# The entry of the gate products: pair 2 moved ahead of the fourth activation sums

## The chip, the cores and the metric

One core of a Trainium2 chip runs the whole kernel as one program. The metric is the device time of one execution in microseconds (us). Five engines matter here: TensorE (PE, with its weight loads as PEld), VectorE (DVE), ScalarE (ACT), GpSimd (POOL), and SyncE (SP), which issues nearly every DMA. Each engine takes its instructions in the order of its own queue.

## The reference

One layer of a hybrid block over 1024 latent tokens and 256 context tokens, all in float32:

```
h  = rms_norm(x, g_pre) * (1 + scale) + shift            # 1024 x 1024
q, k, v, g_a, u_f, g_f, c_a, c_b, g_c, s_a, s_f, s_c = split(h @ w_in)
y_a = (attention(q, k, v, context) * silu(g_a)) @ p_attn
y_f = ((fourier_mix(u_f) @ w_four) * silu(g_f)) @ p_four
y_c = (conv_module(c_a, c_b) * silu(g_c)) @ p_conv
merged = sigmoid(s_a) * y_a + sigmoid(s_f) * y_f + sigmoid(s_c) * y_c
x + gate * rms_norm(merged @ w_out, g_post)
```

The change lies in the products that give the gate columns `s_a`, `s_f`, `s_c`, `g_a`, `g_f`, `g_c`.

## The kernel before

**Split products.** Every float32 operand is written as a high part and a low part (`split`, line 93: ACT casts the high part, DVE or POOL subtracts it to get the low part). A product is then three matmuls per 128 rows of depth: high by high, high by low, low by high (`mm3`, lines 141 to 143).

**Gate pairs.** After the attention stage, the remaining gate columns are computed in twelve pairs, numbered from 0. A pair is 256 columns of `w_in` (two raw tiles of 512 KB, `raw`), and its product with `h` is a 2 by 2 block product done with seven half-size products in place of eight. Each of the seven, `p1` to `p7`, is twelve matmuls of 128x512. They use sums of blocks on both sides:

- on the weight side `prep_a` splits blocks a11 and a12 (tiles `c0`), `wsum(n, 0..3)` forms four sums `w0` to `w3` (line 1283; on POOL for pairs 2 to 11, on DVE for pairs 0 and 1), `prep_b` splits w0 and w1 (tiles `c1`), `prep_c` splits w2 and w3 (tiles `c2`), `prep_d` splits a22 (tile `c3`);
- on the activation side the sums t0 to t3 are formed once for all pairs by `h_sums` and, for the fourth sum set that only `p4` reads, by `h_last` (lines 1243 and 1244). `h_split` splits them. While they wait they are kept in the buffer `mg`.

**Steps of a pair.** `p1` makes bank x and copies it out on ACT (s1, line 1318); `p2` makes bank y; `p6` and then `p7` add onto bank x, each copied out by DVE (u2, u3, line 1320); `p5` makes bank z, copied out by ACT (s5, line 1318), and `p3` adds onto bank z; `p4` makes bank w. Since `p6` adds onto the bank that the s1 copy reads, and `p3` onto the bank that the s5 copy reads, each waits for its copy. The gates `g2`, `g3`, `g4`, `g7` add the pieces on DVE (line 1346), take a tanh on ACT (line 1325, two buffers `th`) and store it by DMA (`thd`).

**Order.** The order on all five engines is that in which the code is written. From pair 3 on a loop emits one pair after another, with the next pair's weights prepared in between. The first three pairs are written out by hand, since the activation sums are formed and split in between. `raws(n)` issues the two loads of a pair's raw tiles, which have two buffers, so they can only start when the former pair's raw tiles have been read for the last time. Six loads of 512 KB (`mg[r]` from `fcd`, line 1483) bring branch results back into `mg` when the sums there have been used up; they too go through SP.

Of the kernel before, what the change touches and what calls it, by code (L numbers as in the profile page):

```python
# [52 lines left out]
def block_kernel(ctx: ExitStack, tc: tile.TileContext, x, ctxt, cvec, cctx, wmodt, wgate,  # L53
                 rows2, cols, w_in, rpbp, w_four, w_pw, pst, w_out, masks, bdc, bds, dcos, dsin, out):
    nc = tc.nc
    pe, act, dve, pool, sp = nc.tensor, nc.scalar, nc.vector, nc.gpsimd, nc.sync
# [35 lines left out]
    def split(src, hi, lo, lo_eng=None):  # L92
        return act.copy(hi, src), (lo_eng or pool).tensor_tensor(out=lo, in0=src, in1=f32(hi), op=ALU.subtract)  # L93
# [10 lines left out]
    def emit_raw(i):  # L104
        while state["raw"] <= min(i, len(wq) - 1):
            e = wq[state["raw"]]
            t = wp.tile([P, e[1], e[2]], F32, tag="raw", bufs=2, name=f"raw{state['raw']}")
            sp.dma_start(t, e[0])
            e[3] = t
            state["raw"] += 1  # L110

    def emit_split(i):
        while state["spl"] <= min(i, len(wq) - 1):
            j = state["spl"]
            emit_raw(j)
            e = wq[j]
            if e[6] == 0:
                state["spl"] += 1
                continue
            e[4] = wp.tile([P, e[1], e[2]], F32R, tag="whi", name=f"whi{j}")  # L120
            e[5] = wp.tile([P, e[1], e[2]], F32R, tag="wlo", name=f"wlo{j}")
            for i in range(e[6]):
                ks = slice(i * e[1] // e[6], (i + 1) * e[1] // e[6])
                lo = e[7][i % len(e[7])] if e[7] else state.get("lo")
                ops = split(e[3][:, ks], e[4][:, ks], e[5][:, ks], lo)
                for op, prev in zip(ops, held):
                    after(op, prev)
            state["spl"] += 1
# [45 lines left out]
    for what in border:  # L174
        n = int(what[1])
# [13 lines left out]
    for what in sum(plan, []) + ["s1"]:  # L189
        n = int(what[1])  # L190
# [136 lines left out]
    def h_split(k, h, eng=None):  # L327
        split(h32s.pop((k, h)), hh[k][:, H[h]], hl[k][:, H[h]], eng)
# [496 lines left out]
    raws = {}  # L825
# [322 lines left out]
    for i in range(NU + 4):  # L1148
        n = i % 16
# [60 lines left out]
    def slot(i, name):  # L1210
        return gp.tile([P, T], F32R, tag=f"g{i}", name=name)
# [12 lines left out]
    def parts(k):  # L1224
        return [[f32(v) for v in bop[i][k]] for i in ((1, 1), 1, (2, 1), (2, 2))]
# [14 lines left out]
    def h_last(k):  # L1240
        b21, l21 = parts(k)[2]
        t2 = ts[4, k] = ts[2, k]
        dve.tensor_tensor(out=t2, in0=b21, in1=t2, op=ALU.subtract)
        dve.tensor_tensor(out=t2, in0=t2, in1=l21, op=ALU.add)  # L1244
# [6 lines left out]
    NP = len(pairs)  # L1251

    def wtile(nm):
        return [wp.tile([P, KT, P], F32R, tag=t, name=nm) for t in ("whi", "wlo")]

    def put(n, name, src, hl_, j):
        dst = [v[:, 4 * j:4 * j + 4] for v in hl_]
        split(src, *dst, dve)
        ops[n, name] = dst

    def blocks(n):
        if n >= NP:
            c0, c1 = ((n - NP + 4 * i) * P for i in range(2))
            return (mgt[0][:, :, c0:c0 + P], mgt[1][:, :, c0:c0 + P],
                    mgt[0][:, :, c1:c1 + P], mgt[1][:, :, c1:c1 + P])
        r0, r1 = (wq[i][3] for i in pairs[n][2])
        return r0[:, 0:4], r0[:, 4:8], r1[:, 0:4], r1[:, 4:8]

    def prep_a(n):
        if n < NP:  # L1270
            emit_raw(pairs[n][2][1])
        a11, a12, _, _ = blocks(n)
        c0 = wtile(f"c0{n}")
        put(n, "a11", a11, c0, 0)
        put(n, "a12", a12, c0, 1)

    def wsum(n, i):
        a11, a12, a21, a22 = blocks(n)
        i0, i1, op = ((a21, a22, ALU.add), (ops.get((n, 0)), a11, ALU.subtract), (a11, a21, ALU.subtract),
                      (a12, ops.get((n, 1)), ALU.subtract))[i]  # L1280
        t = swp.tile([P, 512], F32, tag="sw", name=f"w{i}")
        t = t.rearrange("p (k c) -> p k c", k=4)
        (pool if 1 < n < NP else dve).tensor_tensor(out=t, in0=i0, in1=i1, op=op)  # L1283
        ops[n, i] = t

    def prep_b(n, which=(0, 1)):
        if (n, "c1") not in ops:
            ops[n, "c1"] = [slot(12 + i, f"c1{n}").rearrange("p (k c) -> p k c", k=8) for i in range(2)]
        for i in which:
            put(n, f"s{i + 1}", ops[n, i], ops[n, "c1"], i)  # L1290

    def prep_c(n, which=(0, 1)):
        if (n, "c2") not in ops:
            ops[n, "c2"] = wtile(f"c2{n}")
        for i in which:
            put(n, f"s{3 + i}", ops[n, 2 + i], ops[n, "c2"], i)

    def prep_d(n):
        c3 = (slot(15 if n == 1 else 14, f"c3{n}") if n < NP else hp.tile([P, T], F32R, tag="hh7", name=f"c3{n}"))
        c3 = c3.rearrange("p (k c) -> p k c", k=8)  # L1300
        c3 = c3[:, 0:4], c3[:, 4:8]
        put(n, "a22", blocks(n)[3], c3, 0)

    def raws(n):
        emit_raw(pairs[n - 1][2][1] + 2)
# [112 lines left out]
    for i in (0, 1, 3, 2):  # L1418
        wsum(0, i)
# [8 lines left out]
    def stack_load():  # L1428
        for k in range(8):
            for t, s in zip((hh, hl), H):  # L1430
                sp.dma_start(f32(t[k][:, H[0]]), fcd[k][:, s])

    def stack_in(*ks):
        for k in ks:
            gh.append(slot(order[2 * k], f"gh{k}"))
            gl.append(slot(order[2 * k + 1], f"gl{k}"))
        for t, s in zip((hh, hl), H):
            for k in ks:
                split(f32(t[k][:, H[0]]), gh[k][:, s], gl[k][:, s], dve)

    def go(n, *what):
        for w in what:
            step(n, w)
# [12 lines left out]
    go(0, "p6")  # L1456
    h_split(3, 2, 3)
    wsum(1, 0)
    wsum(1, 1)
    go(0, "p5")  # L1460
    prep_b(1, (1, 0))
# [4 lines left out]
    raws(2)  # L1466
    go(1, "p6", "g2")
    prep_c(1)
    h_last(0)
    go(1, "p5")  # L1470
    h_last(1)
    h_split(4, 0, 1)
    go(0, "g3")
    h_last(2)
    h_last(3)
    h_split(4, 2, 3)
    go(1, "p7")
    prep_a(2)
    go(0, "g7")
    go(1, "p3", "g3")  # L1480
    go(2, "p1", "p2")
    for r in (6, 7, 4, 5, 0, 1):
        sp.dma_start(mg[r], fcd[r])
    wsum(2, 0)
    wsum(2, 1)
    go(0, "p4", "g4")
    prep_b(2)
    go(1, "p4", "g7", "g4")
    prep_d(2)
    wsum(2, 2)  # L1490
    wsum(2, 3)
    prep_c(2)
    raws(3)
    for n in range(2, NP):
        more = n + 1 < NP
        go(n, *("p1", "p2")[2 * (n == 2):], "g2")
        if more:
            prep_a(n + 1)
            wsum(n + 1, 0)
            wsum(n + 1, 1)  # L1500
        else:
            stack_load()
        go(n, "p4")
        if more:
            prep_d(n + 1)
        else:
            stack_in(0, 1, 2)
        go(n, "p6")
        if more:
            wsum(n + 1, 2)  # L1510
            wsum(n + 1, 3)
            raws(n + 2)
        else:
            stack_in(3)
            state["lo"] = dve
            emit_split(i_p[0])
        go(n, "p5")
        if more:
            prep_b(n + 1)
        else:  # L1520
            stack_in(4)
        go(n, "p7", "g7", "g4")
        if not more:
            stack_in(5)
        go(n, "p3", "g3")
        if more:
            prep_c(n + 1)
# [228 lines left out]
    n = NP  # L1756
# [136 lines left out]
```

## Time and profile before

| | |
|---|---|
| median of three runs | 961.87 us (960.55 to 963.34) |
| the profiled execution | 959.82 us, of which the span between the first and last instruction is 958.0 us |
| busy PE / DVE / ACT / POOL | 888.4 / 754.6 / 428.2 / 386.5 us |
| mean granted TensorE clock | 0.98 of full speed |

The span is what the rows below are timed in, from its first instruction on. A busy PE is a PE with a matmul in flight; how fast those go is read from the granted clock beside it.

### The profile page before, as it was taken

The page shows a single profiled execution, that of the slowest core. Times are in us where ns is not written, and L with a number is a line of the kernel's source. Part 1 is how long each engine was busy: PE and PEld are TensorE (multiplying, and loading weights), DVE is VectorE, ACT ScalarE, POOL GpSimd, SP SyncE. Part 2 cuts the span into 40 slices and gives each one's busy share as a digit, 9 for nine tenths or more (in the row PEclk, how much of TensorE's full clock was granted, in tenths as well). Part 3 has the DMA queues.
Part 4 walks back from the last instruction along what each step waited for, and adds up shares of the span by engine and source line. Part 5 has one row for each costly group of instructions (what it writes and reads, how often), then busy time and mean ns, then how long its engine had stood idle before and what let it go on. Part 6 is the DMA issues. An engine that isn't in the chain of part 4 may idle for free. (4 is left out here: it accounts for less than half of the span.)

```text
span 958.0 us, 13133 instructions
## 1 busy us (share of the span) xinstructions
PE 888.4 (93%) x4560; PEld 741.2 (77%) x4560; DVE 754.6 (79%) x1204; ACT 428.2 (45%) x855; POOL 386.5 (40%) x334
## 2 busy tenths in 40 slices
PE   5886999989799999999999968999999999998896
PEld 3655899978578988888888856888778888875685
DVE  5999398989668999999958775447874579998985
ACT  6661522232346767767642433433343430224442
POOL 3694732155214444444520022416653037671232
PEclk9998999999899999999999979999999999999999
DMA  9613123244534454535422246423331599853323
GB/s 354 255 52 104 44 89 134 84 152 125 159 88 123 143 152 130 156 122 144 133 79 88 68 122 216 134 89 99 110 99 44 195 350 327 303 187 110 110 88 132
DMA packets 114308, 136.38 MB, mean 142 GB/s; under 512 B 5697, under 2 KB 83777, under 8 KB 114242
## 3 DMA queue, kind: packets, MB, share of 16 engines
q1 hardware_dynamic: 114098, 134.95, 43.3%
q0 software_dynamic: 144, 0.59, 0.3%
q8 instruction: 36, 0.59, 0.3%
q14 instruction: 30, 0.25, 0.1%
HBM read 102.55 MB, written 29.36 MB: 138 GB/s over the span
## 5 line engine op out<-in xcount | busy, mean ns | idle before, releaser
L141 PE MATMUL ps<-hh,whi 128*128 128x512 f32 x304 | 128.4, 422 | 4.6 <-DVE kst L564 3.7
L143 PE MATMUL ps<-hh,wlo 128*128 128x512 f32 x304 | 120.6, 397 | 0.0
L142 PE MATMUL ps<-hl,whi 128*128 128x512 f32 x304 | 120.4, 396 | 0.0
L93 POOL TENSOR_TENSOR wlo<-raw,whi 128x512 fp32r<-128x512 f32 (+2 forms) x52 | 84.1, 1635 | 77.9 <-ACT whi L93 77.9
L93 DVE TENSOR_TENSOR c<-w,c 128x512 fp32r<-128x512 f32 x64 | 52.8, 862 | 34.4 <-ACT c L93 34.3
L1639 POOL TENSOR_TENSOR mg<-mg,th 128x512 f32<-128x512 f32 x30 | 50.5, 1686 | 62.4 <-DVE th L1636 60.9
L93 ACT CAST whi<-raw 128x512 fp32r<-128x512 f32 (+2 forms) x65 | 43.7, 704 | 66.8 <-PE ps L142 33.5
L141 PEld LDWEIGHTS ps<-hh,whi 128*128 128x128 f32 x304 | 58.7, 193 | 15.2 <-issue 4.6
L1030 POOL TENSOR_TENSOR bias<-mk,braw 128x288 f32<-128x288 bf16 (+1 forms) x64 | 54.1, 847 | 38.4 <-DVE mn L1062 38.4
L143 PEld LDWEIGHTS ps<-hh,wlo 128*128 128x128 f32 x304 | 58.0, 191 | 13.1
L142 PEld LDWEIGHTS ps<-hl,whi 128*128 128x128 f32 x304 | 58.7, 193 | 9.9 <-issue 0.5
L1095 ACT CAST pt<-tp 96x384 fp32r<-96x384 f32 (+1 forms) x96 | 46.1, 514 | 42.9 <-PE tp L1088 42.2
L1283 POOL TENSOR_TENSOR w<-raw 128x512 f32<-128x512 f32 x10 | 16.0, 1601 | 107.0 <-DVE mg L1244 50.3
L1101 DVE TENSOR_TENSOR pt<-tp,pt 96x384 fp32r<-96x384 f32 (+1 forms) x96 | 54.5, 594 | 2.6 <-ACT pt L1095 1.2
L1062 DVE CUSTOM_DVE_ANT_0 pr<-scb,bias 128x544 f32<-128x544 f32 (+1 forms) x64 | 49.4, 772 | 8.5 <-PE scb L1055 7.7
L1069 ACT ACTIVATE pr<-pr,mn 128x544 f32<-128x544 f32 (+1 forms) x64 | 50.8, 794 | 3.7 <-DVE mn L1062 3.6
L143 PE MATMUL ps<-gh,wlo 128*128 128x512 f32 x128 | 50.0, 390 | 0.8 <-DVE wlo L93 0.8
L141 PE MATMUL ps<-gh,whi 128*128 128x512 f32 x128 | 50.2, 392 | 0.0
L142 PE MATMUL ps<-gl,whi 128*128 128x512 f32 x128 | 49.9, 390 | 0.2 <-DVE gl L93 0.2
L1088 PE MATMUL tp<-ident,pr 128*128 128x128 f32 (+1 forms) x320 | 45.8, 274 | 1.4 <-DVE rc L1075 1.0
L93 ACT CAST c<-w 128x512 fp32r<-128x512 f32 x64 | 37.1, 617 | 21.3 <-DVE w L1283 21.1
L1076 DVE TENSOR_SCALAR pr<-pr,rc 128x544 f32<-128x544 f32 (+1 forms) x64 | 41.7, 652 | 2.3
(498 smaller groups left out, 2701.6 us busy)
## 6 DMA issues: line engine op xcount, KB each, us to landing
raw<-in_w_in_dram SPq DMA_DIRECT2D x51, 512.0 KB
wt<-in_wmodt_dram SPq DMA_DIRECT2D x16, 512.0 KB
thd<-th SPq DMA_DIRECT2D x32, 256.0 KB
th<-thd SPq DMA_DIRECT2D x32, 256.0 KB
braw<-in_rpbp_dram SPq DMA_DIRECT2D x32, 192.0 KB
vt<-vd SPq DMA_DIRECT2D x48, 128.0 KB
vd<-vs SPq DMA_DIRECT2D x20, 256.0 KB
vt<-vd SPq DMA_DIRECT2D x48, 96.0 KB
```

The costliest lines, as they stand in the source:

```text
L93: return act.copy(hi, src), (lo_eng or pool).tensor_tensor(out=lo, in0=src, in1=f32(hi), op=ALU.subtract)
L141: pe.matmul(ps, wh, mh, start=start, stop=False, **kw)
L142: pe.matmul(ps, wh, ml, start=False, stop=False, **kw)
L143: pe.matmul(ps, wl, mh, start=False, stop=stop, **kw)
L1030: pool.tensor_tensor(out=dst, in0=mk[:, a * 3 + MJ[j], 0:n].rearrange("p (r w) -> p r w", w=W), in1=raws[h_, min(j, 1)][:, :, 0:W], op=ALU ...
L1062: dve.tensor_tensor_reduce(out=pr, in0=sc, in1=biases[h_][:, FULL[h_](n)], scale=1.0, scalar=BIG, op0=ALU.add, op1=ALU.min, accum_out=mn)
L1069: act.activation(pr, pr, AF.Exp, scale=-1.0, bias=mn, accum_out=sums)
L1076: dve.tensor_scalar(out=pr, in0=pr, scalar1=rc, scalar2=None, op0=ALU.mult)
L1088: pe.transpose(tp[0:(kw if b < 3 else P), b], src, ident)
L1095: act.copy(pt[0:q, b0:b1, 0], tp[0:q, b0:b1])
L1101: dve.tensor_tensor(out=pt[0:q, b0:b1, 1], in0=tp[0:q, b0:b1], in1=f32(pt[0:q, b0:b1, 0]), op=ALU.subtract)
L1639: eng.tensor_tensor(out=mg[d][:, s], in0=mg[d][:, s], in1=t, op=ALU.add)
```

## The change

Three things are done to the stretch between the pair 1 products and pair 3.

- The splits of pair 2 (`prep_a(2)`, then w0, w1 and `prep_b(2)`) move ahead of `h_last` for the fourth activation sums and of `h_split(4, ...)`.
- `p1`, `p2`, `p6` and `p5` of pair 2 move ahead of `p4` of pairs 0 and 1. The rest of pair 2 follows (`p7`, `p4`, `p3`), and its weight preparation and that of pair 3 are written out by hand. The loop starts at pair 3.
- The four weight sums of pair 2 move from POOL to DVE.

No arithmetic is added or removed: the count of matmuls, splits and DMAs is the same.

```
--- before.py
+++ after.py
@@ -1280,7 +1280,7 @@
                       (a12, ops.get((n, 1)), ALU.subtract))[i]
         t = swp.tile([P, 512], F32, tag="sw", name=f"w{i}")
         t = t.rearrange("p (k c) -> p k c", k=4)
-        (pool if 1 < n < NP else dve).tensor_tensor(out=t, in0=i0, in1=i1, op=op)
+        (pool if 2 < n < NP else dve).tensor_tensor(out=t, in0=i0, in1=i1, op=op)
         ops[n, i] = t
 
     def prep_b(n, which=(0, 1)):
@@ -1466,34 +1466,48 @@
     raws(2)
     go(1, "p6", "g2")
     prep_c(1)
+    prep_a(2)
     h_last(0)
     go(1, "p5")
+    wsum(2, 0)
+    wsum(2, 1)
     h_last(1)
+    go(0, "g3")
+    go(1, "p7")
+    prep_b(2, (1, 0))
     h_split(4, 0, 1)
-    go(0, "g3")
+    go(0, "g7")
+    go(1, "p3", "g3")
     h_last(2)
     h_last(3)
+    go(2, "p1", "p2")
     h_split(4, 2, 3)
-    go(1, "p7")
-    prep_a(2)
-    go(0, "g7")
-    go(1, "p3", "g3")
-    go(2, "p1", "p2")
+    go(1, "g7")
     for r in (6, 7, 4, 5, 0, 1):
         sp.dma_start(mg[r], fcd[r])
-    wsum(2, 0)
-    wsum(2, 1)
-    go(0, "p4", "g4")
-    prep_b(2)
-    go(1, "p4", "g7", "g4")
-    prep_d(2)
+    go(2, "p6", "g2")
     wsum(2, 2)
     wsum(2, 3)
+    go(2, "p5")
     prep_c(2)
+    go(0, "p4")
+    prep_d(2)
     raws(3)
-    for n in range(2, NP):
+    go(0, "g4")
+    go(1, "p4", "g4")
+    go(2, "p7")
+    prep_a(3)
+    go(2, "p4", "g7", "g4")
+    for i in range(4):
+        wsum(3, i)
+    prep_d(3)
+    prep_b(3)
+    raws(4)
+    go(2, "p3", "g3")
+    prep_c(3)
+    for n in range(3, NP):
         more = n + 1 < NP
-        go(n, *("p1", "p2")[2 * (n == 2):], "g2")
+        go(n, "p1", "p2", "g2")
         if more:
             prep_a(n + 1)
             wsum(n + 1, 0)
```

**ScalarE, from the splits of w2, w3 of pair 1 on.** In the names, `c21` are the tiles of w2, w3 of pair 1, `c02` the splits of a11, a12 of pair 2, `c12` those of its w0, w1, `t40` and `t41` the high parts of the fourth activation sums, `s1`, `s5` the copies of banks x and z, and `th` a tanh. Before:

```order
L93 CAST c21_6081<-w2_6052 128x512
L93 CAST c21_6081<-w3_6054 128x512
L1318 COPY s5_6102<-z_6089 128x512
L93 CAST t40_5715<-mg1_5697 128x512 x2
L1325 ACTIVATE th_6112<-u2_6009 128x512
L93 CAST t41_5716<-mg0_5696 128x512 x2
L93 CAST c02_6137<-raw35_6059 128x512 x2
L1318 COPY s5_6143<-z_6019 128x512
L1325 ACTIVATE th_6146<-s5_6143 128x512
L1325 ACTIVATE th_6162<-u2_6075 128x512
L1318 COPY s1_6178<-x_6165 128x512
L1325 ACTIVATE th_6217<-u3_6050 128x512
```

and now:

```order
L93 CAST c21_6081<-w2_6052 128x512
L93 CAST c21_6081<-w3_6054 128x512
L93 CAST c02_6087<-raw35_6059 128x512 x2
L1318 COPY s5_6108<-z_6095 128x512
L1325 ACTIVATE th_6118<-u2_6009 128x512
L93 CAST c12_6135<-w1_6112 128x512
L93 CAST c12_6135<-w0_6110 128x512
L93 CAST t40_5715<-mg1_5697 128x512 x2
L1318 COPY s5_6145<-z_6019 128x512
L1325 ACTIVATE th_6148<-s5_6145 128x512
L1325 ACTIVATE th_6164<-u2_6075 128x512
L1318 COPY s1_6184<-x_6171 128x512
```

The splits of pair 2 (`c02`, and now `c12` too) have moved up past both splits `t40` and `t41`. The copy of pair 2's bank x (`s1_6178` before, `s1_6184` now) still stands behind the same two tanhs, the last row of the second piece; ahead of them now also stand the `c12` splits.

**VectorE, at the same place.** `mg1` here holds the fourth activation sums, `c02` and `c12` are the low parts of the splits, `w0` and `w1` pair 2's weight sums, and `u2_6009` is the sum for the gate `g3` of pair 0. Before:

```order
L93 TENSOR_TENSOR c21_6082<-w2_6052,c21_6081 128x512
L93 TENSOR_TENSOR c21_6082<-w3_6054,c21_6081 128x512
L1243 TENSOR_TENSOR mg1_5697<-hh4_87,mg1_5697 128x512
L1244 TENSOR_TENSOR mg1_5697<-mg1_5697,hl4_95 128x512
L1243 TENSOR_TENSOR mg1_5697<-hh5_88,mg1_5697 128x512
L1244 TENSOR_TENSOR mg1_5697<-mg1_5697,hl5_96 128x512
L93 TENSOR_TENSOR t42_5717<-mg1_5697,t40_5715 128x512 x2
L1346 TENSOR_TENSOR u2_6009<-u2_6009,z_6019 128x512
L1346 TENSOR_TENSOR u2_6009<-u2_6009,v_5930 128x512
L1243 TENSOR_TENSOR mg0_5696<-hh6_89,mg0_5696 128x512
L1244 TENSOR_TENSOR mg0_5696<-mg0_5696,hl6_97 128x512
```

and now:

```order
L93 TENSOR_TENSOR c21_6082<-w3_6054,c21_6081 128x512
L93 TENSOR_TENSOR c02_6088<-raw35_6059,c02_6087 128x512 x2
L1243 TENSOR_TENSOR mg1_5697<-hh4_87,mg1_5697 128x512
L1244 TENSOR_TENSOR mg1_5697<-mg1_5697,hl4_95 128x512
L1283 TENSOR_TENSOR w0_6110<-raw36_6061 128x512
L1283 TENSOR_TENSOR w1_6112<-w0_6110,raw35_6059 128x512
L1243 TENSOR_TENSOR mg1_5697<-hh5_88,mg1_5697 128x512
L1244 TENSOR_TENSOR mg1_5697<-mg1_5697,hl5_96 128x512
L1346 TENSOR_TENSOR u2_6009<-u2_6009,z_6019 128x512
L1346 TENSOR_TENSOR u2_6009<-u2_6009,v_5930 128x512
L1320 COPY u3_6133<-x_5961 128x512
L93 TENSOR_TENSOR c12_6136<-w1_6112,c12_6135 128x512
```

Between the splits of pair 1 and the additions into `u2_6009` there now stand the two low parts of `c02` and the two weight sums, while the second half of the fourth sums (`mg0`) and its splits have moved behind.

**TensorE, at the end of `p2` of pair 2** (bank y). `t40` and `t42` are the fourth activation sums, `t20` and `t22` the second ones. Before:

```order
L141 MATMUL y_6180<-hh7_90,c02_6137 128x512
L142 MATMUL y_6180<-hl7_98,c02_6137 128x512
L143 MATMUL y_6180<-hh7_90,c02_6138 128x512
L141 MATMUL w_6203<-t40_5715,c30_5887 128x512
L142 MATMUL w_6203<-t42_5717,c30_5887 128x512
L143 MATMUL w_6203<-t40_5715,c30_5887 128x512
```

and now:

```order
L141 MATMUL y_6186<-hh7_90,c02_6087 128x512
L142 MATMUL y_6186<-hl7_98,c02_6087 128x512
L143 MATMUL y_6186<-hh7_90,c02_6088 128x512
L141 MATMUL x_6171<-t20_5707,c12_6135 128x512
L142 MATMUL x_6171<-t22_5709,c12_6135 128x512
L143 MATMUL x_6171<-t20_5707,c12_6136 128x512
```

Where `p4` of pair 0 (bank w) stood behind `p2`, there now stands `p6` of pair 2, which adds onto bank x of `p1`.

## Rows read from the trace of the kernel before

**Rows 1.** Windows: stretch, us, then busy time of PE, PEld, DVE, ACT, POOL; clock, DMA.
```profile
558.60:566.10 7.50, 0.04 (x1) 0.00 (x0) 7.31 (x10) 2.42 (x5) 3.44 (x3) 0.65 0.09 35
566.10:571.10 5.00, 4.80 (x11) 3.31 (x11) 3.17 (x6) 2.19 (x4) 0.00 (x0) 0.50 0.17 60
...
584.80:588.20 3.40, 3.40 (x10) 2.62 (x9) 0.92 (x2) 0.63 (x1) 0.00 (x0) 0.50 1.03 296
...
640.00:700.00 60.00, 59.56 (x262) 48.72 (x261) 44.98 (x51) 21.53 (x40) 34.50 (x23) 1.00 0.32 101
```

**Rows 2.** Timeline of TensorE: start, us, line, tiles, [idle before <- who ended it].
```profile
555.76 0.39 PE L141 MATMUL z<-hh,c 128*128 128x512 f32 x1
...
566.12 0.80 PE L141 MATMUL x<-hh,c 128*128 128x512 f32 x1 [7.47 <-ACT c L93]
...
583.24 0.50 PE L141 MATMUL w<-t,c 128*128 128x512 f32 x1 [3.33 <-ACT c L93]
...
596.14 0.39 PE L141 MATMUL z<-hh,c 128*128 128x512 f32 x1
...
598.86 0.39 PE L141 MATMUL x<-hh,c 128*128 128x512 f32 x1
```

**Rows 3.** Timeline of ScalarE around the first of these waits.
```profile
551.98 1.12 ACT L93 CAST c<-w 128x512 fp32r<-128x512 f32 x2
553.01 0.57 ACT L1318 COPY s<-z 128x512 f32<-128x512 f32 x1
...
565.45 1.14 ACT L93 CAST c<-raw 128x512 fp32r<-128x512 f32 x2
...
569.30 0.63 ACT L1325 ACTIVATE th<-u 128x512 f32<-128x512 f32 x1
```

**Rows 4.** Timeline of VectorE, same stretch.
```profile
553.83 0.69 DVE L1243 TENSOR_TENSOR mg<-hh,mg 128x512 f32<-128x512 f32 x1
554.55 0.69 DVE L1244 TENSOR_TENSOR mg<-mg,hl 128x512 f32<-128x512 f32 x1
555.15 0.69 DVE L1243 TENSOR_TENSOR mg<-hh,mg 128x512 f32<-128x512 f32 x1
555.88 1.66 DVE L1244 TENSOR_TENSOR mg<-mg,hl 128x512 f32<-128x512 f32 x1
557.46 3.46 DVE L93 TENSOR_TENSOR t<-mg,t 128x512 fp32r<-128x512 f32 x2
```

**Rows 5.** Timeline of GpSimd: first weight sum of pairs 2 and 3.
```profile
555.28 1.71 POOL L1283 TENSOR_TENSOR w<-raw 128x512 f32<-128x512 f32 x1 [50.26 <-DVE mg L1244]
...
590.31 1.43 POOL L1283 TENSOR_TENSOR w<-raw 128x512 f32<-128x512 f32 x1 [28.27 <-DMA raw<-in_w_in_dram]
```

**Rows 6.** Timeline of SP's DMA queue: the raw tiles of pairs 2 and 3, and the six loads.
```profile
549.32 0.99 SPq L108 DMA_DIRECT2D raw<-in_w_in_dram  x2
...
570.60 3.19 SPq L1483 DMA_DIRECT2D mg<-fcd  x6
...
583.13 1.19 SPq L108 DMA_DIRECT2D raw<-in_w_in_dram  x2
```

**Rows 7.** Windows, columns as in rows 1: where those loads end.
```profile
555.00:556.00 1.00, 1.00 (x7) 0.80 (x6) 0.96 (x3) 0.62 (x1) 0.72 (x1) 1.00 0.05 18
...
571.00:581.00 10.00, 8.91 (x39) 6.97 (x38) 2.56 (x4) 2.25 (x4) 0.00 (x0) 0.99 1.01 363
581.00:582.00 1.00, 0.00 (x0) 0.00 (x0) 0.71 (x2) 0.63 (x1) 0.00 (x0) 1.00 0.11 41
```

**Rows 8.** Timeline of TensorE: two shorter waits elsewhere.
```profile
197.52 0.39 PE L142 MATMUL eo<-wlo,ah 128*128 128x256 f32 x1 [2.35 <-POOL wlo L93]
...
868.60 0.50 PE L143 MATMUL y<-wo,c0o 128*128 128x512 f32 x1 [2.43 <-DVE c0o L93]
```

**Rows 9.** Windows, columns as in rows 1: behind those two waits.
```profile
199.00:202.00 3.00, 3.00 (x16) 3.00 (x16) 2.94 (x5) 0.38 (x1) 3.00 (x2) 0.51 0.64 207
...
870.00:874.00 4.00, 4.00 (x20) 3.29 (x19) 3.97 (x6) 2.61 (x4) 0.00 (x0) 1.00 0.13 34
```

## The prediction

> **What bounds the kernel now.** I read the windows first, stretch by stretch, for the granted clock and the busy time of TensorE; then TensorE's timeline, for where it stands still and who ends it; then the other engines' timelines there, for why that engine was late.
>
> From pair 3 on TensorE is never without a matmul for long: 59.56 of 60 us at full clock in a typical stretch of the loop [rows 1]. The stretch before that is where it loses time. The last product of pair 1 starts at 555.76, and a product at full clock takes 2.72 us (two neighbours start at 596.14 and 598.86), so pair 2 could start at 558.48. Nine products lie between there and pair 3's first one at 598.86 [rows 2]. They took 40.4 us; at full clock they need 24.5. So 15.9 us are lost, and that is all a change of order here can win. Two waits make 10.8 of it: 7.47 for the split of pair 2's a11 and a12 by ACT, and 3.33 for the split of its a22 [rows 2]. Behind each the clock is at 0.50 (1.2 in place of 2.4 GHz) while TensorE works, 5.0 us and 3.4 us [rows 1], which costs half of it, 4.2. The last 0.9 are small waits and the modelled ends of matmuls.
>
> Why is the first split late? Not for its data: the two raw tiles are issued at 549.32 and DMA traffic falls to nothing just after 555 [rows 6, 7]. ACT does the split at 565.45 because the fourth activation sums' splits stand ahead of it in its queue [rows 3], and those wait for DVE, which is busy 7.31 of the 7.5 us [rows 1].
>
> **The change, part by part.** I work out when each engine comes to what, from the row at which the two orders part. Durations: an ACT split 0.62, a copy 0.57, a tanh 0.63, followers 0.52 apart (two splits take 1.12 to 1.14) [rows 3]; a DVE subtraction or sum 0.69, starting 0.60 after an independent one and 0.72 after one that it depends on [rows 4].
>
> *The splits of pair 2 go ahead.* ACT is free of pair 1's splits at 553.0 [rows 3]. The first raw tile should be there by about 553.5: an estimate, between half and all of the two tiles' transfer, which ends at 555.05 [rows 7]. Then `c02` is split by 554.6 on ACT and 555.4 on DVE, while `p1` of pair 2 needs it at 558.48. The 7.47 us wait is gone, and the low clock with it. The cover is 3 us. One thing is closer: the copy s5 of pair 1's bank z now stands behind these splits and ends at 555.1 in place of 553.6, and `p3` of pair 1 (555.76) adds onto that bank. If the first tile came only with the second, at 555.05, `p3` would wait 0.9 us.
>
> *What is late next: the copy of bank x.* `p2` of pair 2 ends its issue at 558.48 + 2 x 2.72 = 563.92. Before, `p4` of pairs 0 and 1 stood there and gave ACT 5.4 us. Now `p6` stands there, and it adds onto the bank that the s1 copy must read first. On ACT that copy stands behind a tanh (gate `g3` of pair 0), two `c12` splits, two `t40` splits, a copy and two more tanhs. The first tanh waits for DVE: from 554.15 on DVE has two `c02` subtractions, two sums of `h_last`, the weight sums w0 and w1, two more of `h_last`, and the two additions of the gate, ten instructions at 0.60 to 0.72, which end at 560.7. ACT then runs six instructions at 0.52 to 563.9. The next tanh waits for DVE again (low parts of `c12` and `t40`, an addition) until 565.0, the one after it ends at 566.3, and the copy at 566.8. TensorE so stands still from 563.9 to 566.8, **2.9 us**. From below: nothing, were the copy 2.9 us earlier, for which I see no reason; from above 4.4, if the first raw tile comes at 555.05 and DVE's chain with it. I take 2.9. The `th` buffers are no further wait: the one that the last tanh needs was last written more than 4 us earlier.
>
> *The weight sums on DVE.* Two of the four stand in that chain, 1.3 us of the 2.9. But POOL is then idle, and the rows show what it did to DVE beside it: a sum of 0.69 took 1.66, and a pair of subtractions 3.46 in place of about 1.3 [rows 4], while POOL ran from 555.28 on [rows 5]. That is over 3 us more than the chain would have borne. w2 and w3 (1.3 us) lie after DVE's other work, under `p5` and `p4`.
>
> *Behind the wait.* With `p6` at 566.8, `p5` comes at 569.5, `p4` of pair 0 at 572.3, of pair 1 at 575.0, then `p7`, `p4`, `p3` of pair 2. The fourth sums' last low part, now behind `h_last(2, 3)`, ends on DVE at 569.6: 2.7 us of cover. `c22` is ready at 574.8 for `p7` at 577.7; `c32` waits for `p4` of pair 0 to give up its buffer at 575.0 and is ready at 576.4 for `p4` at 580.4. So the 3.33 us wait goes too, hidden under `p4` of pair 1 and `p7`.
>
> *The low clock.* Behind the 3.33 us wait the clock was low for 3.4 us of work, 1.7 us lost [rows 1, 2]. Of two waits a little shorter than 2.9, one (2.35) has a low clock just behind it and the other (2.43) has not [rows 8, 9]. I take a fall, **1.7 us**; from below nothing, from above 2.5, what the first fall cost (5.0 us of work at half clock).
>
> *The raw tiles of pair 3.* SP issues them behind the six loads of 512 KB. Those need the last fourth-sum splits and stand behind a tanh's store, so they start at about 571.0, as before (570.60), and fill all DMA engines: before, from 571 to just after 581, at 363 GB/s [rows 6, 7]. Now the raw tiles follow at once: a 256 KB store and the first tile pass by about 585.2 at that pace and at that of pair 2's tiles (two in 4.3 us), and `c03` is split by 586.5. (On ACT the tanh of gate `g4` of pair 1 stands ahead of that split, and needs a `th` buffer whose store is queued behind the six loads: it goes at about 583, before the tile is there.) `p1` of pair 3 comes at 587.6, so I take **0**. From above: before, 7.2 us passed between their issue and the first use on POOL [rows 5, 6]. 7.2 us from the end of the six loads, 582.4, plus a split, is 590.3, a wait of 2.7.
>
> *Sum.* Nine products 24.5 + 2.9 + 1.7 = 29.1 in place of 40.4: **11.3 us** won. The profiled execution took 959.82, 1.8 above its span, and becomes 948.5. It lies 2.05 below the median of the three runs, which should go from 961.87 to **950.6**. That the rest of the kernel only shifts rests on the loop being bound by TensorE [rows 1].
>
> [...] Of four waits here three are followed by a low clock, one is not [rows 1, 2, 8, 9]. [...]
>
> **The rivals** (median times).
> - *No fall behind the wait* (25%). Speaks for it: the wait of 2.43 without one. 13.0 us won, perhaps 0.3 given to the raw tiles: 949.
> - *No wait at `p6`* (5%). The chain on DVE and ACT would have to be 2.9 us shorter than its rows. Up to 15.9 won: 946 to 947.5.
> - *The waits are longer* (16%): the first raw tile late, the clock as after the first fall, or pair 3's raw tiles late behind the six loads. All upper ends together leave 15.9 - 4.4 - 2.5 - 2.7 = 6.3 us: 952.5 to 955.5.
> - *Taken back later* (5%): the loop has another bound, so that pair 3 starts early and the end doesn't move. Against it: the row of the loop. 960 to 962.
> - *Slower, by the clock* (4%). If the wait at `p6` leaves the clock at half for the whole stretch, each of the seven products behind it costs 2.72 more, 19 us against the 13.0 won: 968. It decides from 26 us at half clock on. Against it: no stretch behind a wait here was low for more than 5.0 us of work [rows 1].
>
> **Numbers.** The forecast has 45%, its own range 949.5 to 952.5. From no wait at `p6` to the upper ends together the time runs from 947 to 955.5, and about 1 in 10 is left outside on the upper side. A difference of 0.3%, 2.9 us, is what a measurement can tell: faster 91%, same 5%, slower 4%.
>
> **What would show it.** Right: `p1` of pair 2 within 0.3 us of 558.5 with no wait ahead; one wait on ACT's s1 copy at 563.9 of 2 to 4 us; some 3.4 us of clock at 0.50 behind it; no wait at `p4` of pair 2; pair 3 starting at 586 to 589, and the same distance from there to the end as before. Wrong: a wait at `p3` of pair 1 of over 1 us (raw tile late), a wait of pair 3's `p1` on its splits, a low clock longer than 5 us, or an end that moves less than pair 3's start.

## The result and the profile after

The changed kernel takes 952.34 us (median of 5 runs, 950.20 to 958.13), against 962.78 for the kernel before, timed with it: a ratio of 0.9912, 95% interval 0.9887 to 0.9937. It is faster, by 10.4 us by the medians and by 6 to 11 us by the interval.

The traced execution is the slowest of the five, 958.13 us with a span of 956.4, so its end alone would mislead; a second trace of the same kernel (948.96 us) stands in the first experiment. I read both from the same place on, the start of `p3` of pair 1, the last product that the change leaves alone. In the kernel before it is at 555.76 and pair 3 starts at 598.86 [rows 2], 43.10 us later.

TensorE's timeline of the changed kernel:

```profile
556.86 0.39 PE L141 MATMUL z<-hh,c 128*128 128x512 f32 x1
...
559.58 0.39 PE L141 MATMUL x<-hh,c 128*128 128x512 f32 x1
...
568.01 0.50 PE L141 MATMUL x<-t,c 128*128 128x512 f32 x1 [2.82 <-ACT s L1318]
...
587.31 0.50 PE L141 MATMUL x<-hh,c 128*128 128x512 f32 x1
...
598.42 0.50 PE L141 MATMUL x<-t,c 128*128 128x512 f32 x1 [2.40 <-ACT s L1318]
...
606.21 0.50 PE L141 MATMUL x<-t,c 128*128 128x512 f32 x1 [2.04 <-DVE u L1320]
...
613.42 0.39 PE L141 MATMUL x<-hh,c 128*128 128x512 f32 x1
```

The waits of 7.47 and 3.33 us [rows 2] are gone. Pair 2 starts right behind pair 1, one wait of 2.82 us for ACT's copy of bank x stands at its `p6`, and pair 3 starts at 587.31, 30.45 us behind `p3` of pair 1: 12.65 us won up to here. Then come two waits that the kernel before has not, 2.40 us at pair 3's `p6` and 2.04 at its `p7`. The last row is pair 4's first product.

ScalarE's timeline, first at the copy for `p6` of pair 2, then at the first split of pair 3 and the copy for its `p6`; GpSimd's at its first sum of pair 3; and SP's queue (columns as in rows 6):

```profile
566.85 0.63 ACT L1325 ACTIVATE th<-u 128x512 f32<-128x512 f32 x1
567.39 0.57 ACT L1318 COPY s<-x 128x512 f32<-128x512 f32 x1
...
584.96 0.63 ACT L1325 ACTIVATE th<-u 128x512 f32<-128x512 f32 x1 [5.84 <-DMA thd<-th]
586.64 1.14 ACT L93 CAST c<-raw 128x512 fp32r<-128x512 f32 x2 [1.05 <-DMA raw<-in_w_in_dram]
...
597.79 0.58 ACT L1318 COPY s<-x 128x512 f32<-128x512 f32 x1
```

```profile
588.33 1.40 POOL L1283 TENSOR_TENSOR w<-raw 128x512 f32<-128x512 f32 x1 [82.21 <-DMA raw<-in_w_in_dram]
```

```profile
572.58 2.92 SPq L1487 DMA_DIRECT2D mg<-fcd  x6
575.60 0.43 SPq L1326 DMA_DIRECT2D thd<-th  x1
576.12 4.58 SPq L108 DMA_DIRECT2D raw<-in_w_in_dram  x2
```

The first copy stands behind a tanh, as forecast. The next row is the tanh that waits 5.84 us for a store of its buffer, a store that is queued behind the six loads; pair 3's first split follows it, when the raw tile is there. POOL begins pair 3 after TensorE has begun it: 1.0 us behind pair 3's first product, where it stood 8.5 us ahead of it before (590.31 against 598.86) [rows 2, 5].

The clock, from the windows (columns as in rows 1 ahead of the prediction):

```profile
568.00:571.40 3.40, 3.39 (x15) 2.81 (x16) 3.28 (x7) 1.24 (x2) 0.00 (x0) 1.00 0.33 124
...
607.50:610.90 3.40, 3.40 (x10) 2.64 (x9) 0.58 (x2) 0.00 (x0) 0.00 (x0) 0.50 0.91 249
863.50:866.90 3.40, 3.23 (x8) 2.55 (x9) 2.72 (x6) 2.03 (x3) 0.00 (x0) 0.50 0.00 0
901.10:904.50 3.40, 3.40 (x10) 2.63 (x9) 2.51 (x4) 1.24 (x2) 0.61 (x1) 0.50 0.57 201
```

Behind the wait of 2.82 it stays at full speed; behind that of 2.04 it is at 0.50 for 3.4 us, which costs 1.7. Two more such stretches stand near the end, at 863.5 and 901.1, far from anything that the change touches; the trace of the kernel before has none there, though it has waits of nearly the same size at the same two products (2.43 and 2.13 us).

So the span adds up. From pair 3's start to the end it is 369.1 us, before 359.1: 10.0 more, of which the two waits make 4.4 and the three low stretches 5.1. With 12.65 won ahead of them, and a `p3` of pair 1 that came 1.1 later by itself, 1.6 are left, which is 958.0 less 956.4.

### The profile page after: what moved, and what is told of

Read it like the earlier page. It is cut to its first block, busy times and chain, and to the rows that moved or that the text cites. A ratio compares the mean times of both kernels' runs of the same rounds, so it can differ in the third digit from the quotient of the medians.

```text
span 956.4 us, 13130 instructions
## 1 busy us (share of the span) xinstructions
PE 890.5 (93%) x4560; PEld 743.3 (78%) x4560; DVE 757.1 (79%) x1208; ACT 428.2 (45%) x855; POOL 378.6 (40%) x330
## 5 line engine op out<-in xcount | busy, mean ns | idle before, releaser
L1283 POOL TENSOR_TENSOR w<-raw 128x512 f32<-128x512 f32 x9 | 13.9, 1546 | 110.2 <-DMA raw<-in_w_in_dram 100.3
L93 DVE TENSOR_TENSOR c<-raw,c 128x512 fp32r<-128x512 f32 x36 | 36.1, 1042 | 13.8 <-ACT c L93 13.7
```

The costliest lines, as they stand in the source:

```text
L1283: (pool if 2 < n < NP else dve).tensor_tensor(out=t, in0=i0, in1=i1, op=op)
```

## The experiments

All ten were timed beside the kernel before on the same chip. The 95% interval of a ratio here reaches 0.0015 to 0.0027 to either side, about 2 us, so a difference of 2 or 3 us between two rows of the table isn't told by the times alone; there the waits and the clock in the traces carry the reading. "Stage" is the distance from the start of pair 1's `p3` to pair 3's start: 43.10 us before, 27.2 with no loss at all (ten products of 2.72).

| kernel | median us | ratio to before | stage us | waits in pair 2; pair 3 |
|---|---|---|---|---|
| changed | 952.34 | 0.9912 | 30.45 | 2.82; 2.40 and 2.04 |
| changed, again | 952.13 | 0.9910 | 31.74 | 2.65; 0.51 and 1.09 |
| sums on POOL | 955.56 | 0.9934 | 35.77 | 5.45; 0.46 |
| copy first | 955.07 | 0.9929 | 30.96 | none; 3.41, 0.73, 2.17 |
| loads spread | 949.69 | 0.9887 | 31.87 | 2.77; 1.21 |
| copy first, loads spread | 949.12 | 0.9884 | 27.35 | none; 1.99 |
| these two, sums 3 and 4 on DVE | 945.97 | 0.9842 | 27.43 | none; 0.21 |
| before, sums on DVE | 958.33 | 0.9965 | 40.22 | 4.51, 3.24, 1.21; none |
| before, split alone ahead | 963.61 | 1.0024 | 44.97 | 1.50, 0.78, 11.14; none |
| changed, sums 3 and 4 on DVE | 950.35 | 0.9885 | 32.02 | 2.88; none |
| copy first, sums 3 and 4 on DVE | 949.99 | 0.9881 | 31.03 | none; 3.39, 1.15, 0.22 |

**The changed kernel again** (no edit).

> The changed kernel once more, unaltered, for a second trace of it. Theory: the waits of pair 3 in its first trace (2.40 us at p6, 2.04 at p7) belong to the order that the change made, so they stand again within 1 us; the spread of its runs (950.2 to 958.1) comes from low-clock stretches, which can stand at other places; median 950 to 954. Rival: the waits of pair 3 were one execution's accident; then they are gone here and pair 4 starts about 4 us earlier against pair 2's start, and the time is near 949.

TensorE's timeline, the windows of its clock, and ScalarE's timeline at pair 3's first split and at the copy for its `p6`:

```profile
552.76 0.39 PE L141 MATMUL z<-hh,c 128*128 128x512 f32 x1
...
563.72 0.50 PE L141 MATMUL x<-t,c 128*128 128x512 f32 x1 [2.65 <-ACT s L1318]
...
584.50 0.39 PE L141 MATMUL x<-hh,c 128*128 128x512 f32 x1
...
593.33 0.50 PE L141 MATMUL x<-t,c 128*128 128x512 f32 x1 [0.51 <-ACT s L1318]
...
600.16 0.50 PE L141 MATMUL x<-t,c 128*128 128x512 f32 x1 [1.09 <-DVE u L1320]
...
605.74 0.39 PE L141 MATMUL x<-hh,c 128*128 128x512 f32 x1
```

```profile
564.20:567.60 3.40, 3.40 (x10) 2.61 (x9) 2.85 (x5) 1.33 (x3) 0.00 (x0) 0.50 0.19 72
```

```profile
581.55 1.14 ACT L93 CAST c<-raw 128x512 fp32r<-128x512 f32 x2 [1.09 <-DMA raw<-in_w_in_dram]
...
592.70 0.58 ACT L1318 COPY s<-x 128x512 f32<-128x512 f32 x1
```

Both waits of pair 3 stand again, at the same two products and for the same two copies, but smaller: 1.6 us in all in place of 4.4, and the one at `p6` by 1.9 where I expected 1 at most. They belong to the order; their size follows from how far ahead pair 3's splits are. From the first of these splits to the copy for `p6`, ACT and DVE take 11.15 us in both traces (586.64 to 597.79, 581.55 to 592.70). TensorE has three products to do up to `p6`, 8.16 us at full clock. The split began 0.7 us before pair 3's first product in the first trace and 2.95 before it in this one, and the wait is shorter by about as much. This time the clock fell behind the wait at `p6` and not in pair 3; the stage took 31.74, 11.36 less than before. In these two traces a fall in the stage thus costs less than its 1.7 us in the end: part of what TensorE loses there it waits less at pair 3. From pair 3 to the end it is 362.7, 3.6 more than before: the two waits, and one low stretch of 1.7 near the end. The two traces of one program differ by 9.2 us: 6.4 behind pair 3's start (2.8 of waits and two low stretches more in the first), 4.1 ahead of the change, less 1.3 in the stage.

**Pair 2's sums on POOL.**

```
-        (pool if 2 < n < NP else dve).tensor_tensor(out=t, in0=i0, in1=i1, op=op)
+        (pool if 1 < n < NP else dve).tensor_tensor(out=t, in0=i0, in1=i1, op=op)
```

> The changed kernel with pair 2's four weight sums back on POOL, the order kept. Theory (the sums belong on DVE here, because POOL slows DVE beside it): DVE loses 1.4 us of sums but its h_last and gate additions take up to 3 us more beside POOL, so the wait at pair 2's p6 grows from 2.8 to 4 to 5 us, with a low clock behind it: 1 to 4 us slower than the changed kernel. Rival (the order alone does it, the engine is indifferent): wait within 0.7 us of 2.8 and the same time within 1 us.

VectorE's timeline from `h_last` on, then GpSimd's:

```profile
554.32 1.78 DVE L1243 TENSOR_TENSOR mg<-hh,mg 128x512 f32<-128x512 f32 x1
556.13 1.67 DVE L1244 TENSOR_TENSOR mg<-mg,hl 128x512 f32<-128x512 f32 x1
557.72 1.78 DVE L1243 TENSOR_TENSOR mg<-hh,mg 128x512 f32<-128x512 f32 x1
559.53 1.67 DVE L1244 TENSOR_TENSOR mg<-mg,hl 128x512 f32<-128x512 f32 x1
```

```profile
555.62 1.62 POOL L1283 TENSOR_TENSOR w<-w,raw 128x512 f32<-128x512 f32 x1
557.21 1.74 POOL L1283 TENSOR_TENSOR w<-raw,raw 128x512 f32<-128x512 f32 x1
```

Beside POOL each of the four sums takes 1.67 to 1.78 us in place of 0.69, so the copy of bank x comes later, the wait at `p6` is 5.45, the clock behind it is low for 6.0 us of work, and the kernel is 3.2 us slower than the changed one by the medians. That is the way the theory went; the wait is somewhat above the 4 to 5 us that it gave, and since pair 3's preparation is then further ahead, only 0.46 us of waits are left there. The Trainium skill (SBUF — State Buffer, section "Who interferes with whom") says that a VectorE instruction with both inputs in SBUF contends with a GpSimd one that reads SBUF. The trace agrees, and gives the size: each of the four takes about as long as the POOL instruction beside it.

**The copy of bank x first on ACT.**

```
-    go(0, "g7")
-    go(1, "p3", "g3")
+    go(1, "p3")
+    go(2, "p1", "p2")
+    go(1, "g3")
+    go(0, "g7")
     h_last(2)
     h_last(3)
-    go(2, "p1", "p2")
```

> The changed kernel with p1 and p2 of pair 2 written ahead of the gates g7 of pair 0 and g3 of pair 1, so that ACT's copy of bank x stands ahead of their two tanhs; the order on TensorE is unchanged. Theory: the wait of 2.8 us at pair 2's p6 falls to under 0.5 us, but pair 3's raw tiles are still queued behind the six loads, so p1 of pair 3 now waits 1.5 to 3 us for its splits and little reaches the end: within 1.5 us of the changed kernel. Rival (pair 3's raw tiles have slack): pair 3 starts 2.8 us earlier and the whole is 2.5 to 4.5 us faster than the changed kernel.

TensorE's timeline, then ScalarE's:

```profile
586.00 0.50 PE L141 MATMUL x<-hh,c 128*128 128x512 f32 x1 [3.41 <-ACT c L93]
...
604.99 0.50 PE L141 MATMUL x<-t,c 128*128 128x512 f32 x1 [2.17 <-DVE u L1320]
```

```profile
583.66 0.63 ACT L1325 ACTIVATE th<-u 128x512 f32<-128x512 f32 x1 [6.66 <-DMA thd<-th]
585.33 1.14 ACT L93 CAST c<-raw 128x512 fp32r<-128x512 f32 x2 [1.03 <-DMA raw<-in_w_in_dram]
```

The wait at pair 2's `p6` is gone and comes back whole, as 3.41 us at pair 3's first product. ACT waits there first for a store queued behind the six loads, and then for the raw tile behind that. At pair 3's `p7` 2.17 us stand as well, for the copy u2. The mechanism is as expected. The median is 2.7 us above the changed kernel's, outside the 1.5 that I gave it, and the clock fell behind the new wait; but the runs of the two overlap widely (950.43 to 956.95 and 948.96 to 958.13), so a loss isn't shown; the gain of 2.5 to 4.5 that the rival gave isn't there.

**The six loads spread.**

```
-    for r in (6, 7, 4, 5, 0, 1):
-        sp.dma_start(mg[r], fcd[r])
+    def mg_load(*rs):
+        for r in rs:
+            sp.dma_start(mg[r], fcd[r])
...
     raws(3)
+    mg_load(6, 7)
...
     raws(4)
+    mg_load(4, 5)
...
             raws(n + 2)
+            if n == 3:
+                mg_load(0, 1)
```

> The changed kernel with the six loads into mg issued two at a time behind the raw tiles of pairs 3, 4 and 5 in place of all six ahead of pair 3's. Theory (pair 3's waits come from raw tiles and a store that are queued behind the six loads): pair 3's raw tiles land some 4 to 6 us earlier, the wait at its p6 (2.40) is gone or under 0.5, that at its p7 (2.04) shrinks too: 3 to 6 us faster than the changed kernel, 945 to 949. Rival (the waits come from ACT's and DVE's own order and from POOL beside DVE): the splits of pair 3 come earlier but the copy of its bank x does not, waits stay within 1 us, and the time is the same within 1.5 us.

2.7 us faster than the changed kernel by the medians, somewhat under the 3 to 6 expected and not clear of the noise (intervals 0.9862 to 0.9912 and 0.9887 to 0.9937). GpSimd's timeline:

```profile
582.88 1.30 POOL L1283 TENSOR_TENSOR w<-raw 128x512 f32<-128x512 f32 x1 [77.88 <-DMA raw<-in_w_in_dram]
```

POOL's first sum of pair 3 now stands 4.8 us ahead of pair 3's first product (587.64), where it was 1.0 behind it in the changed kernel's first trace and 1.2 ahead in the second. The wait at pair 3's `p6` is gone. The clock fell in the stage here, as in the second trace, so its 0.51 is what this compares with, rather than 2.40. The wait at `p7` stays, 1.21: for that one the loads are not the cause.

**Both.**

> Both together: ACT's copy of bank x ahead of the two tanhs, and the six loads spread behind the raw tiles of pairs 3, 4 and 5. Theory (the copy's 2.8 us were lost again only because pair 3's raw tiles stood behind the six loads): no wait over 0.5 us at pair 2's p6 and none over 1 us at pair 3's p1, pair 3 starts 27.5 to 28.5 us behind the start of pair 1's p3, and the time is 2 to 5 us below that of spread loads alone (949.7). Rival (pair 3's preparation is late for another reason, its chain of raw tiles, POOL sums and splits): a wait of 2 us or more stands at pair 3's p1, p6 or p7 and the time is within 1.5 us of 949.7.

Its stage is 27.35 us: next to nothing is lost any more between pair 1 and pair 3. But the time is within the noise that of spread loads alone. TensorE's timeline:

```profile
600.56 0.64 PE L141 MATMUL x<-t,c 128*128 128x512 f32 x1 [1.99 <-DVE u L1320]
```

The rival was right: a wait of 1.99 at pair 3's `p7`, with a low clock behind it. VectorE's timeline ahead of it, and GpSimd's:

```profile
594.92 4.99 DVE L93 TENSOR_TENSOR c<-raw,c 128x512 fp32r<-128x512 f32 x3 [1.21 <-ACT c L93]
599.83 0.68 DVE L1320 COPY u<-x 128x512 f32<-128x512 f32 x1
```

```profile
594.68 1.30 POOL L1283 TENSOR_TENSOR w<-raw 128x512 f32<-128x512 f32 x1 [6.49 <-DMA raw<-in_w_in_dram]
...
599.32 1.72 POOL L1283 TENSOR_TENSOR w<-raw,w 128x512 f32<-128x512 f32 x1
```

Three low parts of pair 4, two SBUF inputs each, take 4.99 us beside POOL's sums of the same pair. The copy u2 that `p7` needs stands behind them. It itself takes 0.68 beside POOL's last sum, as it does with POOL idle (last row of the next trace): it reads TensorE's bank. The same section of the Trainium skill says that a VectorE instruction with at most one SBUF input, outside its 2-port modes, does not contend with GpSimd; the trace agrees.

**The sums of pairs 3 and 4 on DVE**, with both edits above, with neither, and with the copy alone.

```
-        (pool if 2 < n < NP else dve).tensor_tensor(out=t, in0=i0, in1=i1, op=op)
+        (pool if 4 < n < NP else dve).tensor_tensor(out=t, in0=i0, in1=i1, op=op)
```

> As the kernel with both edits, and the weight sums of pairs 3 and 4 on DVE too. Theory (the wait at pair 3's p7 for the copy u2 comes from POOL's sums of pair 4 beside DVE's splits of the same pair): the wait at p7 of pair 3 is gone and the time 1 to 3 us below the kernel with both edits. Rival (DVE is simply full there, eight sums of 0.69 us more make it later): a wait of 1 us or more at p6 or p7 of pairs 3 or 4, and the time the same or up to 3 us above.

> The changed kernel with the weight sums of pairs 3 and 4 on DVE, and nothing else. Theory (what pair 3 gave back came from POOL's sums beside DVE): the waits at pair 3's p6 and p7 (2.40 and 2.04 us in one trace, 0.51 and 1.09 in the other) fall to under 0.5 each; 2 to 5 us faster than the changed kernel (952.3), 947 to 950. Rival (it came from pair 3's raw tiles behind the six loads): a wait of 0.5 us or more stays at p6 and the time is within 1.5 us of 952.3.

> The copy of bank x ahead and the sums of pairs 3 and 4 on DVE, with the six loads left ahead of pair 3's raw tiles. Theory (the loads are what the earlier pair 3 runs into): a wait of 2 to 4 us at pair 3's p1 as with the copy alone, a low clock behind it, and none at its p6 and p7; 949 to 952, some 4 us above the kernel that has the loads spread too (946.0). Rival (with the sums on DVE the loads cost nothing): no wait at p1, within 1.5 us of 946.0.

With both edits: of the waits in pairs 2 and 3 only 0.21 us at `p7` is left, and the time is 945.97 us, 3.2 below both edits alone and the fastest of all (0.9842, interval 0.9817 to 0.9867). VectorE's timeline at the same place as above:

```profile
594.64 1.29 DVE L93 TENSOR_TENSOR c<-raw,c 128x512 fp32r<-128x512 f32 x2 [1.21 <-ACT c L93]
595.86 0.68 DVE L1283 TENSOR_TENSOR w<-raw 128x512 f32<-128x512 f32 x1
596.57 0.69 DVE L1283 TENSOR_TENSOR w<-w,raw 128x512 f32<-128x512 f32 x1
597.18 0.68 DVE L93 TENSOR_TENSOR c<-raw,c 128x512 fp32r<-128x512 f32 x1
597.78 0.68 DVE L1320 COPY u<-x 128x512 f32<-128x512 f32 x1
```

Though two sums now stand in between, the copy starts 3.1 us after the first of the low parts (597.78 less 594.64) in place of 4.9 (599.83 less 594.92). With neither edit, which is the changed kernel with these sums on DVE: both waits of pair 3 are gone, though the loads stand where they did; from the first split of pair 3 to the copy for `p6` ACT and DVE now take 9.9 us in place of 11.15. By the medians it is 2.0 us faster, the low end of what the theory gave and not clear of the noise. Its trace has the fall in the stage too, so the waits that went are the 1.6 us of the second trace and not 4.4. So in these traces either edit removes the wait at `p6`: it took both, raw tiles that came late and sums that slowed the preparation. With the copy alone: the wait at pair 3's `p1` stands again, 3.39, as the theory said, since the loads are still ahead of the raw tiles, and the time, 949.99, is 4.0 above that of the kernel with the loads spread too (948.56 to 953.43 against 943.75 to 948.94); the wait at `p6`, 1.15, it had not foreseen, and the low clock that it expected behind the one at `p1` did not come.

**The kernel before, with DVE sums for pair 2 only.**

> The kernel before with one part of the change alone: pair 2's four weight sums on DVE, the order as before. Theory (POOL's sums slow DVE's splits of the fourth activation sums, which hold up pair 2's first split): DVE runs that stretch 3 us faster, the wait of 7.47 us falls to 4 to 5, the one of 3.33 stays; 2.5 to 5 us faster than before. Rival (only the order matters): the 7.47 us stay within 1 us and so does the time.

3.4 us faster than before (1.5 to 5.2 by the interval); TensorE's timeline has the first wait at 4.51 in place of 7.47, the second almost as it was, and a new one of 1.21 stands at pair 2's `p7`:

```profile
563.88 0.79 PE L141 MATMUL x<-hh,c 128*128 128x512 f32 x1 [4.51 <-ACT c L93]
...
581.21 0.50 PE L141 MATMUL w<-t,c 128*128 128x512 f32 x1 [3.24 <-ACT c L93]
```

So about a third of the gain, by the medians, comes from the engine of four instructions, through DVE's other work.

**The kernel before, with the first split moved only.** `prep_a(2)` stands behind `prep_c(1)`, all else as before.

```
     prep_c(1)
+    prep_a(2)
     h_last(0)
...
     go(1, "p7")
-    prep_a(2)
     go(0, "g7")
```

> The kernel before with another part alone: the split of pair 2's a11 and a12 ahead of the fourth activation sums, the products in the order of before and the sums on POOL. Theory (the split alone only moves the wait, since p4 of pair 0 then comes before the fourth sums are split): no wait at pair 2's p1, but 3 to 5 us at p4 of pair 0 and some 3 us at p4 of pair 2; 3 to 6 us faster than before. Rival (the late split was the whole loss): no wait over 1 us at p4 of pair 0 and 8 us or more faster.

1.9 us slower than before. The wait at `p1` is gone, at `p4` of pair 0 it is 2.3 in all, but at `p4` of pair 2 it is 11.14 and not 3. Timelines of TensorE, of ScalarE and of SP's queue:

```profile
587.05 0.79 PE L141 MATMUL w<-t,c 128*128 128x512 f32 x1 [11.14 <-ACT c L93]
```

```profile
585.86 0.63 ACT L1325 ACTIVATE th<-u 128x512 f32<-128x512 f32 x1 [7.22 <-DMA thd<-th]
586.40 0.60 ACT L93 CAST c<-raw 128x512 fp32r<-128x512 f32 x1
```

```profile
573.78 3.09 SPq L1483 DMA_DIRECT2D mg<-fcd  x6
```

The products come sooner, the six loads do not. The tanh of gate `g4` of pair 1 needs a buffer whose store is queued behind them; ACT waits 7.22 us for it, and the split for `p4` stands behind that tanh. The changed kernel has the same tanh, waiting for the same reason, but with `p5`, `p4` and `p7` in front of TensorE meanwhile. So neither expectation held, and the split alone wins nothing: by the interval it loses 0.9 to 3.8 us.

## Why the prediction was right, and where it was not

The time, 952.34, lies in the range, 1.7 above the forecast and 0.2 below its upper end. That it does is partly luck: a term was left out, what it costs differs between executions, and of the five runs two lie above the range (954.28 and 958.13). Up to pair 4's first product, which the forecast moves by the same 11.3 us as all that follows, 5.6 us were won in the first trace and 9.2 in the second: 62.1 us behind `p3` of pair 1 before, 56.6 and 53.0 after. The row of before:

```profile
617.90 0.39 PE L141 MATMUL x<-hh,c 128*128 128x512 f32 x1
```

Point by point:

- *The two waits go, pair 2 starts at once*: right, 2.72 us behind `p3` in the trace.
- *A wait of 2.9 at `p6` for the copy of bank x*: right, 2.82 and 2.65, with the chain that was worked out: the last tanh ends at 567.5 and the copy at 568.0, where the forecast had 566.3 and 566.8; 1.1 of that is `p3` of pair 1, which came later by as much. That it is this chain the kernel with the copy first shows.
- *A fall of the clock behind it, 1.7*: it came in one trace and not in the other. It came in the two further kernels that have the same wait, too (2.77 with the loads spread, 2.88 with the sums of pairs 3 and 4 on DVE, each with 3.4 us of work at 0.50 behind it): three of four. So the stage won 12.65 or 11.36 where 11.3 was forecast and 13.0 in the rival.
- *Sums on DVE beside an idle POOL*: right, by the kernel with the sums on POOL and by that of before with the sums on DVE.
- *The raw tiles of pair 3, a wait of 0*: right at `p1`, in the first trace with nothing to spare: its split began at 586.64, where the forecast had it done by 586.5. The kernel with the copy first shows a wait as soon as TensorE comes 2.8 us sooner.
- *"The rest of the kernel only shifts"*: this step failed. It rested on the row of the loop, in which TensorE is never without a matmul for long. That row holds for a loop whose preparation is ahead. POOL's first sum of pair 3 stood 8.5 us ahead of pair 3's first product before, and 1.0 behind it after: TensorE came to it 11.6 us sooner, POOL only 2.0. So ACT's copy for pair 3's `p6` now comes at the end of preparation that starts too late for it, 11.15 us behind the first split, and DVE's copy for `p7` stands behind three low parts of pair 4 on which POOL's sums of that pair now fall. They took 2.36 us before and 5.07 now. The loss was 4.4 us and a fall in one trace, 1.6 in the other. That these two are the causes the kernels with the loads spread and with the sums of pairs 3 and 4 on DVE show. The prediction's own sign for it came true: the end moved less than pair 3's start, 369.1 and 362.7 us from there to the end in place of 359.1 (of which 3.4 and 1.7 are low stretches near the end). The rival "taken back later" named it, at its full size and with 5%; as a part of the gain it belonged in the sum.

VectorE's rows for those three low parts, before and then now, with the copy for `p7` behind them:

```profile
606.64 2.36 DVE L93 TENSOR_TENSOR c<-raw,c 128x512 fp32r<-128x512 f32 x3 [1.21 <-ACT c L93]
```

```profile
600.49 5.07 DVE L93 TENSOR_TENSOR c<-raw,c 128x512 fp32r<-128x512 f32 x3 [1.21 <-ACT c L93]
605.48 0.68 DVE L1320 COPY u<-x 128x512 f32<-128x512 f32 x1
```

The term that was left out is thus worth 1.6 to 6.1 us in waits and clock, and the term of the fall 0 to 1.7. They are not independent: the trace with the fall in the stage has the smaller loss behind it.

## What to carry to other kernels

A stretch that wins time for one engine delivers it to a loop whose preparation keeps its own pace, by transfers and a slower engine: ask of the first turns how far ahead their data are, in microseconds, and take off what the gain exceeds that by. When an operation is moved between engines, price what it does to the engine beside it, not only its own duration. A load that is needed late but queued early holds up the stores and loads behind it: in the changed kernel's two traces six such loads made a tanh wait 5.84 and 3.40 us for its buffer's store. Spreading them was worth 2.7 us by the medians, not clear of the noise, and 4.0 where the copy first and the sums on DVE left TensorE nothing else to wait for.

## What the runs showed of the hardware

The first thing is that waits of one size are followed by a low clock in one execution and not in another: behind 2.82 us at the same product the clock stayed full, behind 2.65 it fell for 3.4 us, and near the end two places fall in one trace, one in another and none in a third. At pair 3's first product it fell behind 3.41 us (copy first) and not behind 3.39 (copy first, sums on DVE). Each such stretch of 3.4 us at 0.50 costs TensorE 1.7 us. The trace of the kernel before has none near its end, which fits its 959.82 lying below its median.

The second is the price of two engines reading SBUF at once: a VectorE sum of 0.69 us took 1.67 to 1.78 beside a GpSimd sum, and three low parts took 4.99, against an estimate of 1.9 without POOL (two took 1.29, and each that follows adds 0.60).
